# Four units of seven products instead of three in two steps of an FFN, and partial sums added by transfers into DRAM

## The chip, the cores and the metric

The kernel runs on one core of a Trainium2 chip. The core has five engines with queues of their own: TensorE (PE, matrix products), VectorE (DVE), ScalarE (ACT), GpSimd (POOL) and SyncE (SP, which here only issues transfers); transfers are carried by 16 DMA engines. Products are summed in PSUM, everything else lives in SBUF or in DRAM. The metric is the device time of one launch in microseconds (us); less is better.

## What is computed

One layer of an encoder on 256 tokens of width 2048, in fp32: a mixing part (attention heads and a recurrence, behind one input and one output projection), a gated FFN of inner width 5632, and a gated per-layer embedding. The change lies in the FFN:

```
fn = rms_norm(h, g_ffn_pre)
ff = (silu(fn @ w_ffn_gate) * (fn @ w_ffn_up)) @ w_ffn_down
h = h + rms_norm(ff, g_ffn_post)
```

## The kernel before

**Precision.** Every weight product is made of three matmuls on fp32r operands: each operand is split into a high and a low part, and high·high, low·high and high·low are summed. A weight tile (128 x 1024, two blocks of the inner dimension, 512 columns each) is loaded by SP (`wr`, `third`, `lower`, `ple` are its homes, by the ring it comes from), ACT casts its high part (L640, `wh`), DVE takes the low part as the difference (L653, `wl`), and PE uses both (L691 to L693, in this order for each block). The activations hF are split once, at the start of the FFN. High and low parts have rings of four tiles, so DVE can be at most some tiles ahead of PE: how far it is ahead is called its lead in what follows.

**Steps.** The inner width of 5632 is done in 11 steps of 512 columns (f = 0 to 10), in three parts: steps 0 to 3, 4 to 7 and 8 to 10. A step makes two chunks, gate and up, each over eight pairs of blocks k = 0, 2, ..., 14 of fn. ACT then applies silu to the gate (L1725), DVE multiplies by the up product (L1744) and transposes (L340) into a tile `mid`, and 16 small transfers (L350) on POOL, for the last step of a part half of them on SP, arrange it as `mT`. ACT and DVE split it (L312, L314) into `mid0`, `mid1`, `mid2`, one per part. After a part come its down products: four chunks c over the part's inner columns.

**Seven products.** A unit is one pair of k of the gate and the up chunk: eight products of [128 x 128] by [128 x 512], of three matmuls each, 24 matmuls. In steps 2 to 10, for k = 0, 2, 4 (`SEVEN_KS`), the eight are replaced by seven products of sums, in the manner of Strassen and Winograd: 21 matmuls (L702 to L704). They come in three pieces: `four_products` (two tiles of half the usual work, 12 matmuls), begun while the step in front still runs, `two_products` and `one_product`. The sums of weights are DVE's: L588, L592 and L598 in `sum_stream`; the last addend of a block is fetched by an adding transfer on POOL (L609), which waits for the tile's low part. The sums of activations are made once per k (L798, L805 and a split). When the fours of all units of a step are done, `made_of_four` turns the four accumulators into what the rest is added to: a copy on ACT (L750) of one accumulator, then L752, L754, L757 and L759 on DVE.

**Part sums.** The down products of part one are copied to `mid` tiles (ACT, L1832) and stored to a DRAM tensor, part 0. Those of part two are added by DVE (L1825) to what POOL loads back (L1818), and stored to part 1 (L1835). Part three adds its own to `mg`, which SP reloads from part 1 (L1848) near the end of step 10.

**Order.** The program is unrolled. PE's order is written by the groups: the table `FOURS` says at which pair of a step each `four_products` of the next is put, and `TAKEN` when its own twos and ones come. Where the work of the other engines stands in their queues is set by a planner, which keeps a clock for each engine from a table of costs and puts each piece where it expects its inputs; each engine then works through its queue in that order and waits where an input is late.

Of the kernel before, what the change touches and what calls it, by code (L numbers as in the profile page):

```python
# [10 lines left out]
F32 = mybir.dt.float32  # L11
# [5 lines left out]
P = 128  # L17
S = 256
# [22 lines left out]
DOWN_KS = (0, 2, 4, 6)  # L41
OUT = (3, 6, 7, 1)
SEVEN_F = range(2, 11)

SWAPPED = [
    (lambda f: (("w_ffn_gate", f), ("w_ffn_up", f)), SEVEN_F, SEVEN_KS),
    *(
        (
            lambda c: (("w_ffn_down", c), ("w_ffn_down", c + 1)),
# [191 lines left out]
def layer(ctx: ExitStack, tc: tile.TileContext, a: dict, out: bass.AP):  # L241
# [130 lines left out]
    def done(event):  # L372
        event.t = plan.now
# [11 lines left out]
    class Act:  # L385
# [51 lines left out]
    class Group:  # L437
# [76 lines left out]
                fours[self.own[j]] = (*x, self.twos[j])  # L514

    TAKEN = {
        "up3": ("", "01", "2ab"), "down4": ("", "ab0", "12", "3"), "down2": ("", "01", "a"),
    }
    FOURS = {
        ("up0", "up3"): (3, 5, 7), ("up3", "up3"): (2, 3, 4), ("up3", "down4"): (2, 3, 3, 4),  # L520
        ("down4", "down4"): (1, 2, 3, 3), ("down4", "up3"): (1, 2, 3), ("up3", "down2"): (4, 4), ("down2", "down2"): (2, 3),
    }
    fours = {}
# [50 lines left out]
    def sum_stream():  # L574

        for i in sorted(fours):
            for e in fours[i][4].values():
                yield e
            late, last, j, js, _, two = fours[i]
            n, b = first_slot[i], OUT[j]  # L580
            b0 = 2 - 2 * n
            yield ev_load[i]
            yield ev_load[i + 1]
            if n or j == 3:
                yield ev_half_spilled
            Q, R = loaded.pop(i), loaded.pop(i + 1)
            yield dve(N, take=f"T{n}")
            nc.vector.tensor_tensor(  # L588
                out=blocks()[:, b0, :], in0=Q[:, 0, :], in1=Q[:, 1, :], op=ALU.add
            )  # L590
            yield dve(N, take=f"t{j}")
            nc.vector.tensor_tensor(  # L592
                out=blocks()[:, b, :], in0=blocks()[:, b0, :], in1=R[:, 1, :], op=ALU.add
            )
            raws[i] = blocks()[:, b0 : b + 1 : b - b0, :]
            done(ev_raw[i, 2])
            yield dve(N)
            nc.vector.tensor_tensor(out=Q[:, 1, :], in0=Q[:, 1, :], in1=R[:, 1, :], op=ALU.add)  # L598
            raws[i + 1], raws[two] = Q, R
            done(ev_raw[i + 1, 2])  # L600
            done(ev_raw[two, 2])
# [113 lines left out]
    def four_products(group, j, i):  # L715
        (C1, _, _), (C2, _, _) = group.chunks
        kx = group.sevens[j][1]
        ev_s = group.lhs.ev_sums[kx]
        first, last = j == 0, j == len(group.sevens) - 1
        if first:  # L720
            C1.open()
            C2.open()
        plan.main(0, ev_lo[i, 2], group.lhs.ev[kx], ev_s, C1.ready, C2.ready)
        s = group.lhs.sums[kx]
        product(C2.accs[0], s["S1"], i, 0, first, last)
        product(C2.accs[1], s["S2"], i, 1, first, last)
# [58 lines left out]

    def sums_of(lhs, kx, hi, lo):

        lhs.sums[kx] = {
            n: (hi[:, i * P : (i + 1) * P], lo[:, i * P : (i + 1) * P])
            for i, n in enumerate(("S1", "S2", "S7", "S4"))  # L790
        }
        yield lhs.ev[kx]
        yield lhs.ev[kx + 1]
        for j in range(2):
            h, l = lhs.at[kx + j]
            yield dve(S, take=None if j else "T4")
            e, f = (t2["ple"][:, 1, c : c + N] for c in (D // 2, D // 2 + N))
            nc.vector.tensor_tensor(  # L798
                out=e[:, j * S : (j + 1) * S], in0=f32(h), in1=f32(l), op=ALU.add
            )  # L800
        a11, a21, a12, a22 = (e[:, i * P : (i + 1) * P] for i in range(4))
        s1, s2, s7, s4 = (f[:, i * P : (i + 1) * P] for i in range(4))
        for dst, x, y in ((s1, a21, a22), (s2, a11, s1), (s7, a21, a11), (s4, a12, s2)):
            yield dve(P)
            nc.vector.tensor_tensor(out=dst, in0=x, in1=y, op=ALU.subtract)  # L805
        yield from split(hi, lo, f, N, give="T4")
        done(lhs.ev_sums[kx])

    def more_sums():
        for e in hF.ev:  # L810
            yield e
        t2["s"] = t2["pool"].tile([P, 4, N], F32R, tag="mg1", name="s")
        done(ev_unmerged)
        yield from sums_of(hF, 4, t2["s"][:, 0, :], t2["s"][:, 1, :])
        for e in hF.ev_sums.values():
            yield e
        for j in range(4):
            plan.free[f"t{j}"].append(plan.now)
# [183 lines left out]

    HB = 4
    mixT = Act()
    ssr = const.tile([P, S], F32, name="ssr")
    ssa = const.tile([P, S], F32, name="ssa")

    def second_tiles():
        plan.reach(ev_x)
# [145 lines left out]
    def group_rstd(ss, name):  # L1155

        yield pe(0.44, take="sm")
        pb = bank(f"pb_{name}")
        nc.tensor.matmul(pb[:, 0, :], ones, ss, start=True, stop=True)
        rb = const.tile([P, S], F32, name=f"rb_{name}")  # L1160
# [439 lines left out]
    def split_turned(c, mT, hi, lo, nxt, gname):  # L1600
        for b in range(4):
# [10 lines left out]
    parts = [  # L1612
        ctx.enter_context(
            tc.tile_pool(name=f"parts{i}", bufs=1, space=bass.MemoryType.DRAM)
        ).tile([NT, P, D], F32, name=f"part{i}")
        for i in range(2)
    ]
    ev_spilled, ev_all_spilled, ev_back = Event(), Event(), Event()

    def spill_h():  # L1620
# [110 lines left out]
    def mid_tile():  # L1731
        return t2["pool"].tile([P, NT, N], F32, tag="mid", name="mid", bufs=2)
# [79 lines left out]
    def down_post(part, c):  # L1812
        def post(ch):
            sl = slice(c * N, (c + 1) * N)
            if part:
                yield ("pool", COST["move"], None, "mid", None)
                e, here = mid_tile(), Event()
                nc.gpsimd.dma_start(e, parts[0].rearrange("t p d -> p t d")[:, :, sl])  # L1818
                plan.now += COST["landing"]
                done(here)  # L1820
                yield here
            for t in range(NT):
                if part:
                    yield dve(N)
                    nc.vector.tensor_tensor(  # L1825
                        out=e[:, t, :], in0=ch.accs[t], in1=e[:, t, :], op=ALU.add
                    )
                else:
                    yield act(N, take=None if t else "mid")
                    if not t:  # L1830
                        e = mid_tile()
                    nc.scalar.copy(e[:, t, :], ch.accs[t])  # L1832
            ch.release()
            yield ("pool", COST["move"], None, None, None)
            nc.gpsimd.dma_start(parts[part].rearrange("t p d -> p t d")[:, :, sl], e)  # L1835
            plan.now += COST["landing"]
            plan.free["mid"].append(plan.now)
            ev_parts.append((part, c))
        return post
# [35 lines left out]
    for part, (f0, f1) in enumerate(PARTS):  # L1875
        mid = Mid(f"mid{part}")
        last_part = part == len(PARTS) - 1
        for f in range(f0, f1):
            slot = ring()
            g = Chunk(gate_post(f), slot=slot)  # L1880
            u = Chunk(up_post(f, mid, (f - f0) * 4, g, f == f1 - 1), late=(-3 if f == f1 - 1 else -1) * SOON, slot=slot)
            groups.append(Group(
                [(g, "w_ffn_gate", f * N), (u, "w_ffn_up", f * N)], hF, KS,
                SEVEN_KS if f in SEVEN_F else (),
            ))
        ks = [(f0 * 4 + k, k) for k in range(0, (f1 - f0) * 4, 2)]
        for c in range(0, 4, 2):
# [326 lines left out]
```

## Time and profile before

| | |
|---|---|
| median of three runs | 1147.19 us (1147.03 to 1148.57) |
| the profiled execution | 1146.92 us, its span 1145.1 us |
| FFN gate and up, down, in the trace | about 360 to 1036 us |
| matmul records | 5193, of which 15 fp32 matmuls are recorded twice |
| TensorE clock granted | 0.998 |
| memory traffic | 249.65 MB read, 9.44 MB written |

A row of the profile names line, engine, operation, output and inputs, shape and count; times are us from the start of the span, and in a timeline the start, then the duration. Idle time before an instruction stands in brackets with what ended it. Matmuls overlap, so their price is the distance of starts and not the duration of a row.

### The profile page before, as it was taken

To read this page: it belongs to the slowest core of one execution; us is meant where nothing else is said; L and a number is where in the kernel's file an instruction comes from. 1 tells how busy PE (TensorE), PEld (TensorE's weight loads), DVE (VectorE), ACT (ScalarE), POOL (GpSimd) and SP (SyncE) were. 2 spreads that over 40 slices of the span, in tenths; PEclk is the share of its full clock that TensorE was granted. 3 is DMA by queue.
4 is the path that set the end of the run, shared out by engine and by line. 5 is a ranking of instruction groups with operands and counts; after the bars stand their busy time and mean duration, and the time that the engine had idled before them with its cause. 6 is when DMAs were issued, how large, how long until landed. Compare 5 with 4: busy or idle time off the path is not lost.

```text
span 1145.1 us, 15184 instructions
## 1 busy us (share of the span) xinstructions
PE 1136.3 (99%) x5193; PEld 944.7 (82%) x5193; DVE 932.7 (81%) x1174; ACT 727.2 (63%) x959; POOL 147.7 (13%) x234
## 2 busy tenths in 40 slices
PE   9999999999999999999999999999999999999997
PEld 8888888888888888888888888888888888788886
DVE  6678697888468779898987898999988888888574
ACT  6877877875447645665666566556555565577564
POOL 0000000000000032132010133222111303100200
PEclk9999999999999999999999999999999999999999
DMA  9867566546685996887977777897797777977861
GB/s 317 295 191 217 182 193 200 175 150 203 220 300 175 314 295 207 228 243 214 292 259 220 257 225 214 249 274 240 257 317 246 216 249 240 278 237 257 240 218 74
DMA packets 110558, 268.49 MB, mean 234 GB/s; under 512 B 36304, under 2 KB 43216, under 8 KB 109072
## 3 DMA queue, kind: packets, MB, share of 16 engines
q1 hardware_dynamic: 96304, 243.17, 63.3%
q0 software_dynamic: 13744, 24.00, 10.9%
q8 instruction: 40, 0.66, 0.2%
q10 hardware_dynamic: 432, 0.35, 0.1%
q14 instruction: 38, 0.31, 0.1%
HBM read 249.65 MB, written 9.44 MB: 226 GB/s over the span
## 4 chain that ended last, share of the span: by engine, by line
PE 93%; DVE 3%; DMA 2%; ACT 2%; issue 1%; SPq 0%; POOL 0%; ACTq 0%; DVEq 0%; POOLq 0%
PE acc L693 23%; PE acc L692 23%; PE acc L691 23%; PE acc L704 6%; PE acc L703 6%; PE acc L702 6%; DVE wl L653 1%; PE tr L331 1%; DMA mg<-part 1%; ACT wh L640 1%; DMA sq<-ev 0%; PE warm L2123 0%; PE pg L362 0%; PE pg L363 0%; PE pg L361 0%
## 5 line engine op out<-in xcount | busy, mean ns | idle before, releaser
L653 DVE TENSOR_TENSOR wl<-wr,wh 128x1024 fp32r<-128x1024 f32 (+1 forms) x300 | 358.6, 1209 | 100.7 <-ACT wh L640 98.9
L640 ACT CAST wh<-wr 128x1024 fp32r<-128x1024 f32 (+1 forms) x300 | 310.8, 1043 | 171.8 <-PE acc L692 114.2
L350 POOL DMA_DIRECT2D mT<-mid x164 | 96.3, 597 | 607.7 <-DMA lower<-in_w_ffn_up 400.7
L692 PE MATMUL acc<-wh,hT_mix_lo 128*128 128x512 f32 x420 | 163.6, 390 | 0.3 <-DVE hT_mix_lo L320 0.3
L691 PE MATMUL acc<-wh,hT_mix_hi 128*128 128x512 f32 x420 | 163.7, 390 | 0.0
L693 PE MATMUL acc<-wl,hT_mix_hi 128*128 128x512 f32 x420 | 163.4, 389 | 0.0
L693 PE MATMUL acc<-wl,hT_hi 128*128 128x512 f32 x320 | 124.6, 390 | 0.0
L691 PE MATMUL acc<-wh,hT_hi 128*128 128x512 f32 x316 | 124.4, 394 | 0.0
L692 PE MATMUL acc<-wh,hT_lo 128*128 128x512 f32 x316 | 123.1, 390 | 0.0
L640 ACT CAST wh<-ple 128x1024 fp32r<-128x1024 f32 (+1 forms) x68 | 68.2, 1008 | 77.2 <-DVE ple L592 47.3
L692 PEld LDWEIGHTS acc<-wh,hT_mix_lo 128*128 128x128 f32 x420 | 78.9, 188 | 17.2 <-DVE hT_mix_lo L320 1.0
L691 PEld LDWEIGHTS acc<-wh,hT_mix_hi 128*128 128x128 f32 x420 | 78.9, 188 | 16.3
L693 PEld LDWEIGHTS acc<-wl,hT_mix_hi 128*128 128x128 f32 x420 | 78.8, 188 | 16.3
L653 DVE TENSOR_TENSOR wl<-ple,wh 128x1024 fp32r<-128x1024 f32 (+1 forms) x68 | 79.2, 1164 | 10.1 <-ACT wh L640 9.7
L693 PEld LDWEIGHTS acc<-wl,hT_hi 128*128 128x128 f32 x320 | 60.1, 188 | 13.0 <-DVE wl L653 0.3
L692 PEld LDWEIGHTS acc<-wh,hT_lo 128*128 128x128 f32 x316 | 59.4, 188 | 11.6
L691 PEld LDWEIGHTS acc<-wh,hT_hi 128*128 128x128 f32 x316 | 59.4, 188 | 11.5
L609 POOL DMA_DIRECT2D ple<-in_w_ffn_up x27 | 24.0, 890 | 164.6 <-DVE wl L653 123.2
L640 ACT CAST wh<-third 128x1024 fp32r<-128x1024 f32 x32 | 33.6, 1051 | 13.4 <-PE acc L692 7.9
L691 PE MATMUL acc<-wh,hT_ffn_hi 128*128 128x512 f32 x104 | 40.9, 393 | 0.0
L692 PE MATMUL acc<-wh,hT_ffn_lo 128*128 128x512 f32 x104 | 40.6, 390 | 0.1
L693 PE MATMUL acc<-wl,hT_ffn_hi 128*128 128x512 f32 x104 | 40.5, 390 | 0.0
(439 smaller groups left out, 2455.6 us busy)
## 6 DMA issues: line engine op xcount, KB each, us to landing
wr<-in_w_in SPq DMA_DIRECT2D x77, 512.0 KB, 4.5
wr<-in_w_ffn_gate SPq DMA_DIRECT2D x73, 512.0 KB, 5.3
wr<-in_w_ffn_down SPq DMA_DIRECT2D x55, 512.0 KB, 6.0
wr<-in_w_ffn_up SPq DMA_DIRECT2D x51, 512.0 KB, 4.8
wr<-in_w_out SPq DMA_DIRECT2D x32, 512.0 KB, 4.3
wr<-in_w_ple_gate SPq DMA_DIRECT2D x32, 512.0 KB, 4.6
lower<-in_w_ffn_up SPq DMA_DIRECT2D x21, 512.0 KB, 6.1
lower<-in_w_ffn_down SPq DMA_DIRECT2D x17, 512.0 KB, 5.5
```

What stands on the lines that cost most here:

```text
L331: nc.tensor.transpose(tr[:, b, t * P : (t + 1) * P], e[:, t, sl], ident)
L350: (nc.gpsimd if i in pool else nc.sync).dma_start(dst[32 * j : 32 * j + 32, :, :, i, :], src[32 * i : 32 * i + 32, :, :, j, :],)
L609: nc.gpsimd.dma_start(dst, src, accum_op=ALU.add)
L640: nc.scalar.copy(his[i][:, 0 : src.shape[1], :] if n == 2 else his[i][:, j, :], src)
L653: nc.vector.tensor_tensor(out=los[i][:, m, :], in0=src, in1=f32(his[i][:, m, :]), op=ALU.subtract)
L691: nc.tensor.matmul(accs[t], hi[:, sl], his[i][:, j, :], start=st, stop=False, **group)
L692: nc.tensor.matmul(accs[t], lo[:, sl], his[i][:, j, :], start=False, stop=False, **group)
L693: nc.tensor.matmul(accs[t], hi[:, sl], los[i][:, j, :], start=False, stop=sp, **group)
L702: nc.tensor.matmul(dst, x[0], wh, start=start, stop=False, skip_group_check=seeded)
L703: nc.tensor.matmul(dst, x[1], wh, start=False, stop=False, skip_group_check=seeded)
L704: nc.tensor.matmul(dst, x[0], wl, start=False, stop=stop, skip_group_check=seeded)
```

## The change

The units of k = 6 of steps 5 and 9 are made of seven products too. The sums of hF for k = 6 get a tile `more`, which takes a place where small statistics of the mixing part lay before (`ssr`, `ssa`, `rb_*`, now together in `quad`). A step with four units takes its fours at pairs 2, 2, 3, 3 of the step in front instead of 2, 3, 4, and begins those of the next step at pairs 1, 2, 3 instead of 2, 3, 4. For the fourth unit the block sums take another slot, so the order of blocks within a tile is turned there (`turn`).

The four down products of part two are no longer added by DVE: ACT copies them to `mid`, as in part one, and POOL's transfer adds them in DRAM to what part one has stored. One DRAM tensor `parted` takes the place of the two.

```diff
+FOUR_F = (5, 9)
 SWAPPED = [
     (lambda f: (("w_ffn_gate", f), ("w_ffn_up", f)), SEVEN_F, SEVEN_KS),
+    (lambda f: (("w_ffn_gate", f), ("w_ffn_up", f)), FOUR_F, (6,)),
...
     TAKEN = {
-        "up3": ("", "01", "2ab"), "down4": ("", "ab0", "12", "3"), "down2": ("", "01", "a"),
+        "up3": ("", "01", "2ab"), "up4": ("", "ab0", "12", "3"), "down4": ("", "ab0", "12", "3"), "down2": ("", "01", "a"),
     }
     FOURS = {
         ("up0", "up3"): (3, 5, 7), ("up3", "up3"): (2, 3, 4), ("up3", "down4"): (2, 3, 3, 4),
+        ("up3", "up4"): (2, 2, 3, 3), ("up4", "up3"): (1, 2, 3), ("up4", "down4"): (1, 2, 3, 3),
+        ("up4", "up4"): (1, 2, 3, 3), ("down4", "up4"): (1, 2, 3, 3), ("up4", "down2"): (2, 3),
...
-            raws[i] = blocks()[:, b0 : b + 1 : b - b0, :]
+            raws[i] = blocks()[:, min(b, b0) : max(b, b0) + 1 : abs(b - b0), :]
...
-        product(C2.accs[0], s["S1"], i, 0, first, last)
-        product(C2.accs[1], s["S2"], i, 1, first, last)
+        turn = int(OUT[j] < 2 - 2 * first_slot[i])
+        product(C2.accs[0], s["S1"], i, turn, first, last)
+        product(C2.accs[1], s["S2"], i, 1 - turn, first, last)
...
+        more = const.tile([P, 4, S], F32R, tag="quad", name="more")
+        yield from sums_of(hF, 6, *(more[:, :, b : b + P] for b in (0, P)))
...
-    ssr = const.tile([P, S], F32, name="ssr")
-    ssa = const.tile([P, S], F32, name="ssa")
+    quad = const.tile([P, 4, S], F32, tag="quad", name="quad")
+    ssr, ssa = quad[:, 0, :], quad[:, 1, :]
...
-            if part:
-                yield ("pool", COST["move"], None, "mid", None)
-                e, here = mid_tile(), Event()
-                nc.gpsimd.dma_start(e, parts[0].rearrange("t p d -> p t d")[:, :, sl])
-                plan.now += COST["landing"]
-                done(here)
-                yield here
             for t in range(NT):
-                if part:
-                    yield dve(N)
-                    nc.vector.tensor_tensor(
-                        out=e[:, t, :], in0=ch.accs[t], in1=e[:, t, :], op=ALU.add
-                    )
-                else:
-                    yield act(N, take=None if t else "mid")
-                    if not t:
-                        e = mid_tile()
-                    nc.scalar.copy(e[:, t, :], ch.accs[t])
+                yield act(N, take=None if t else "mid")
+                if not t:
+                    e = mid_tile()
+                nc.scalar.copy(e[:, t, :], ch.accs[t])
             ch.release()
             yield ("pool", COST["move"], None, None, None)
-            nc.gpsimd.dma_start(parts[part].rearrange("t p d -> p t d")[:, :, sl], e)
-            plan.now += COST["landing"]
+            to = parted.rearrange("t p d -> p t d")[:, :, sl]
+            if part:
+                nc.gpsimd.dma_start(to, e, accum_op=ALU.add)
+                plan.now += ADDED
+            else:
+                nc.gpsimd.dma_start(to, e)
+                plan.now += COST["landing"]
...
-        nc.sync.dma_start(back[n, t], (spill if n == "h" else parts[1])[t])
+        nc.sync.dma_start(back[n, t], (spill if n == "h" else parted)[t])
...
-                SEVEN_KS if f in SEVEN_F else (),
+                SEVEN_KS + (6,) if f in FOUR_F else SEVEN_KS if f in SEVEN_F else (),
```

The planner's clocks run differently with this, so other work changes its place as well, from step 4 on; the program has 6 matmuls fewer. Three places follow.

DVE in step 10, around the sums that follow the fours of the down products of part three (L752 to L759, after the change L757 to L764), the low parts (L653, then L657) of the last tiles of step 10 beside them, and the up product's post (L1744 and L340, then L1747 and L342). Before:

```order
L314 TENSOR_TENSOR mid2l_7832<-mT,mid2h_7831 128x512 x2
L653 TENSOR_TENSOR wl<-third,wh 128x1024
L653 TENSOR_TENSOR wl<-wr,wh 128x1024 x2
L752 TENSOR_TENSOR u<-u,acc_8286 128x512
L754 TENSOR_TENSOR u<-u,acc_8284 128x512
L757 TENSOR_TENSOR acc_8286<-acc_8285,u 128x512
L759 TENSOR_TENSOR acc_8285<-acc_8285,u 128x512
L653 TENSOR_TENSOR wl<-wr,wh 128x1024 x2
L1744 SCALAR_TENSOR_TENSOR mid<-acc_7866,rstd_f,mid 128x512
L1744 SCALAR_TENSOR_TENSOR mid<-acc_7867,rstd_f,mid 128x512
L340 STREAM_TRANSPOSE mid<-mid 128x1024
```

After the change:

```order
L316 TENSOR_TENSOR mid2l_7869<-mT,mid2h_7868 128x512 x2
L657 TENSOR_TENSOR wl<-wr,wh 128x1024
L757 TENSOR_TENSOR u<-u,acc_8290 128x512
L759 TENSOR_TENSOR u<-u,acc_8288 128x512
L762 TENSOR_TENSOR acc_8290<-acc_8289,u 128x512
L764 TENSOR_TENSOR acc_8289<-acc_8289,u 128x512
L657 TENSOR_TENSOR wl<-third,wh 128x1024
L657 TENSOR_TENSOR wl<-wr,wh 128x1024 x2
L657 TENSOR_TENSOR wl<-lower_3672,wh 128x1024
L1747 SCALAR_TENSOR_TENSOR mid<-acc_7833,rstd_f,mid 128x512
L1747 SCALAR_TENSOR_TENSOR mid<-acc_7834,rstd_f,mid 128x512
L342 STREAM_TRANSPOSE mid<-mid 128x1024
```

The sums stand one low part earlier: the first one behind them (from `third`) is now that of the last up tile of step 10, which stood ahead of them before. The post has four low parts between itself and the sums, where it had two.

POOL from the down products of part two to the moves of step 8: loads and stores of the part sums, late weight additions for steps 8, 9 and 10 (into `ple`), moves of mT. Before:

```order
L1818 DMA mid<-part_98 128x2x512 x2
L1835 DMA part_101<-mid 128x2x512
L609 DMA ple<-in_w_ffn_up 128x512
L1835 DMA part_101<-mid 128x2x512
L609 DMA ple<-in_w_ffn_up 128x512 x2
L1818 DMA mid<-part_98 128x2x512 x2
L1835 DMA part_101<-mid 128x2x512 x2
L609 DMA ple<-in_w_ffn_up 128x512 x3
L350 DMA mT<-mid 32x8x32 x16
```

After the change:

```order
L1827 DMA parted<-mid 128x2x512 x2
L613 DMA ple<-in_w_ffn_up 128x512 x3
L1827 DMA parted<-mid 128x2x512 x2
L613 DMA ple<-in_w_ffn_up 128x512 x4
L352 DMA mT<-mid 32x8x32 x9
L613 DMA ple<-in_w_ffn_up 128x512
L352 DMA mT<-mid 32x8x32 x7
```

The loads are gone, the stores of a pair of chunks stand together, a fourth late addition follows them, and one for the step after stands between the ninth and the tenth move of mT.

PE in step 4, from the second tile of the third unit of fours of step 5 (on `s`, the sums of hF for k = 4; L702 to L704 are the seven products, L691 to L693 the plain ones, after the change L706 to L708 and L695 to L697). Before:

```order
L702 MATMUL acc_5524<-wh,hT_mix_hi 128x512
L703 MATMUL acc_5524<-wh,hT_mix_lo 128x512
L704 MATMUL acc_5524<-wl,hT_mix_hi 128x512
L702 MATMUL acc_5525<-wh,s 128x512
L703 MATMUL acc_5525<-wh,s 128x512
L704 MATMUL acc_5525<-wl,s 128x512
L691 MATMUL acc_5173<-wh,hT_mix_hi 128x512
L692 MATMUL acc_5173<-wh,hT_mix_lo 128x512
L693 MATMUL acc_5173<-wl,hT_mix_hi 128x512
```

After the change:

```order
L706 MATMUL acc_5527<-wh,hT_mix_hi 128x512
L707 MATMUL acc_5527<-wh,hT_mix_lo 128x512
L708 MATMUL acc_5527<-wl,hT_mix_hi 128x512
L706 MATMUL acc_5528<-wh,s 128x512
L707 MATMUL acc_5528<-wh,s 128x512
L708 MATMUL acc_5528<-wl,s 128x512
L706 MATMUL acc_5529<-w,more 128x512
L707 MATMUL acc_5529<-w,more 128x512
L708 MATMUL acc_5529<-w,more 128x512
L706 MATMUL acc_5530<-w,more 128x512
```

The fourth unit (on `more`) follows the third at once, and the second follows the first in the same way: four weight tiles of six matmuls stand back to back, where each unit of fours had tiles of twelve matmuls behind it.

More of the change, by code (lines that the diff above doesn't have):

```diff
@@ L786, in sums_of @@
     def sums_of(lhs, kx, hi, lo):
[L788 to L791, printed above, removed]
+        if len(hi.shape) == 2:
+            hi, lo = (x.rearrange("p (b q) -> p b q", q=P) for x in (hi, lo))
+        lhs.sums[kx] = {n: (hi[:, i, :], lo[:, i, :]) for i, n in enumerate(("S1", "S2", "S7", "S4"))}
         yield lhs.ev[kx]
@@ L805, in sums_of @@
             nc.vector.tensor_tensor(out=dst, in0=x, in1=y, op=ALU.subtract)
-        yield from split(hi, lo, f, N, give="T4")
+        yield from split(hi, lo, f.rearrange("p (b q) -> p b q", q=P), N, give="T4")
         done(lhs.ev_sums[kx])
@@ L1159, in group_rstd @@
         nc.tensor.matmul(pb[:, 0, :], ones, ss, start=True, stop=True)
-        rb = const.tile([P, S], F32, name=f"rb_{name}")
+        rb = quad[:, 2 if name == "rec" else 3, :]
         yield act(S, SQRT, give="sm")
@@ L1611, in layer @@
     ).tile([NT, P, D], F32, name="h_spill")
[L1612 to L1617, printed above, removed]
+    parted = ctx.enter_context(
+        tc.tile_pool(name="parted", bufs=1, space=bass.MemoryType.DRAM)
+    ).tile([NT, P, D], F32, name="parted")
     ev_spilled, ev_all_spilled, ev_back = Event(), Event(), Event()
```

## Prediction

> **What bounds the kernel now.** I read the page first: busy time by engine, and the chain of waits.
>
> ```profile
> span 1145.1 us, 15184 instructions
> ...
> PE 1136.3 (99%) x5193; PEld 944.7 (82%) x5193; DVE 932.7 (81%) x1174; ACT 727.2 (63%) x959; POOL 147.7 (13%) x234
> ...
> PE 93%; DVE 3%; DMA 2%; ACT 2%; issue 1%; SPq 0%; POOL 0%; ACTq 0%; DVEq 0%; POOLq 0%
> ```
>
> TensorE sets the time: 99% busy, 93% of the chain. So the time changes by two things alone: the number of matmuls, and the holes in PE's stream that other engines make. The price of a matmul comes from the timeline of PE in step 10:
>
> ```profile
> 975.61 0.39 PE L704 MATMUL acc<-wl,sums 128*128 128x512 f32 x1
> 975.84 0.39 PE L691 MATMUL acc<-wh,hT_mix_hi 128*128 128x512 f32 x1
> ...
> 978.56 0.39 PE L691 MATMUL acc<-wh,hT_mix_hi 128*128 128x512 f32 x1
> ...
> 979.01 0.39 PE L693 MATMUL acc<-wl,hT_mix_hi 128*128 128x512 f32 x1
> ```
>
> From 975.84 to 978.56 PE starts the 12 matmuls of one weight tile: 2.72 us, 0.2267 us each, whatever the 0.39 of a single row says. Holes: from step 0 to the end of the FFN I find one of note, in the down products of part three.
>
> ```profile
> 996.47 0.39 PE L703 MATMUL acc<-wh,sums 128*128 128x512 f32 x1
> 997.03 0.50 PE L704 MATMUL acc<-wl,sums 128*128 128x512 f32 x1 [0.18 <-DVE wl L653]
> 997.37 0.40 PE L702 MATMUL acc<-wh,sums 128*128 128x512 f32 x1
> ...
> 998.32 0.39 PE L703 MATMUL acc<-wh,mid2l 128*128 128x512 f32 x1
> 998.77 0.50 PE L704 MATMUL acc<-wl,mid2h 128*128 128x512 f32 x1
> 999.10 0.40 PE L702 MATMUL acc<-wh,sums 128*128 128x512 f32 x1
> ...
> 994.79 0.69 DVE L314 TENSOR_TENSOR mid2l<-mT,mid2h 128x512 fp32r<-128x512 f32 x1 [3.10 <-ACT mid2h L312]
> ...
> 981.48 9.73 DMA mg<-part
> ...
> 991.23 2.81 DMA mT<-mid
> ```
>
> Starts 0.56 (996.47 to 997.03), 0.34, 0.45 (998.32 to 998.77) and 0.33 apart instead of 0.2267: 1.68 - 4 x 0.2267 = 0.77 us, and some 0.85 with the 0.24 steps beside them. The chain names its origin: the reload of `mg` takes from 981.48 to 991.23, the last transfer that turns the activations of step 10 (mT) goes behind it, and DVE stands 3.10 us for it.
>
> So DVE is the engine to watch. What matters is not its share but its lead: by how much the low part of a weight tile (L653) is done before PE starts on the tile.
>
> ```profile
> 653.00:695.00 42.00, 42.00 (x188) 34.76 (x186) 37.80 (x44) 25.61 (x29) 12.00 (x19) 1.00 0.73 223
> 902.00:944.00 42.00, 42.00 (x187) 34.80 (x186) 36.42 (x41) 24.41 (x28) 12.06 (x19) 1.00 0.73 223
> ...
> 646.46 1.22 DVE L653 TENSOR_TENSOR wl<-wr,wh 128x1024 fp32r<-128x1024 f32 x1 [1.49 <-ACT wh L640]
> ...
> 653.52 0.39 PE L691 MATMUL acc<-wh,hT_mix_hi 128*128 128x512 f32 x1
> ...
> 713.55 1.22 DVE L653 TENSOR_TENSOR wl<-third,wh 128x1024 fp32r<-128x1024 f32 x1
> ...
> 714.72 0.39 PE L691 MATMUL acc<-wh,hT_mix_hi 128*128 128x512 f32 x1
> ```
>
> The first two rows are windows of 42 us over steps 5 and 9 (columns: sum, PE, PEld, DVE, ACT, POOL, clock, DMA share, GB/s): DVE works 37.8 and 36.4 us of each. The tile that PE starts at 653.52 was ready at 646.46 + 1.22 = 647.68, 5.8 us ahead; the ring of four tile buffers allows no more. The one started at 714.72, in step 6, was ready at 714.77: no lead at all, and no hole only because `wl` is read by the third matmul of the tile.
>
> **The change, part by part.** *Matmuls.* Steps 5 and 9 each turn one unit of eight products (24 matmuls) into seven (21): 2 x 3 = 6 matmuls fewer, 6 x 0.2267 = **-1.36 us**. Nothing excludes it, since PE streams without holes there. The Trainium skill, "TensorE: Matmul & The Clock Gate", section "Back-to-back issue gap", puts a sustained matmul of 512 columns at about 131 ns; by it the six would be worth 0.79 us, estimated. The trace disagrees (226.7 ns), and the trace decides.
>
> *DVE's new work.*
>
> ```profile
> L592 DVE TENSOR_TENSOR ple<-ple,lower 128x512 f32<-128x512 f32 x38 | 26.2, 690 | 1.2 <-DMA lower<-in_w_ffn_up 0.3
> L588 DVE TENSOR_TENSOR ple<-wr 128x512 f32<-128x512 f32 x37 | 25.1, 678 | 0.0
> L598 DVE TENSOR_TENSOR wr<-wr,lower 128x512 f32<-128x512 f32 x31 | 21.2, 685 | 0.0
> ...
> L1825 DVE TENSOR_TENSOR mid<-acc,mid 128x512 f32<-128x512 f32 x8 | 5.2, 683 | 0.0
> ...
> L805 DVE TENSOR_TENSOR ple<-ple 128x128 f32<-128x128 f32 x12 | 2.9, 286 | 0.1
> L798 DVE TENSOR_TENSOR ple<-hT_mix_hi,hT_mix_lo 128x256 f32<-128x256 f32 x6 | 2.4, 415 | 0.0
> ```
>
> A unit of seven adds, over the pair it replaces, three sums (0.68 + 0.69 + 0.69 = 2.05), one more full low part (1.22, as at 646.46) and half a one (0.54 over the half tile): 3.8 us, while PE needs 0.68 less. Step 5's window becomes 37.8 + 3.8 = 41.6 of 41.3 us. That is more than full, but part of it is done in step 4, whose tiles lead by nearly the whole 5.8, and steps 6 and 10 begin their own fours one pair earlier. Going through the new order tile by tile with these durations, I find the lead never under 0.8 us in steps 4 to 6 and 8 to 9: at the four tiles done back to back (1.8), after the sums of the four (0.8 to 1.4, where the tile's first two matmuls give 0.45 more), and at the up product's end. I take 0; bounds 0 and, if the lead is gone in both places, the 5.2 of the first slow rival. The sums of activations for k = 6 (two of L798, four of L805, one split of 0.68: 2.7 us) fall before step 2, with the ring's lead to cover them: 0.
>
> *Step 10, up product.* Here the order puts the sums that follow the fours (L752 to L759) one tile earlier.
>
> ```profile
> 974.45 1.06 ACT L640 CAST wh<-wr 128x1024 fp32r<-128x1024 f32 x1 [0.30 <-PE acc L703]
> 975.41 0.57 ACT L750 COPY u<-acc 128x512 f32<-128x512 f32 x1
> ...
> 972.86 2.54 DVE L653 TENSOR_TENSOR wl<-wr,wh 128x1024 fp32r<-128x1024 f32 x2
> 976.02 0.69 DVE L752 TENSOR_TENSOR u<-u,acc 128x512 f32<-128x512 f32 x1 [0.61 <-ACT u L750]
> ...
> 978.14 0.69 DVE L759 TENSOR_TENSOR acc<-acc,u 128x512 f32<-128x512 f32 x1
> 978.74 2.35 DVE L653 TENSOR_TENSOR wl<-wr,wh 128x1024 fp32r<-128x1024 f32 x2
> 981.00 1.41 DVE L1744 SCALAR_TENSOR_TENSOR mid<-acc,rstd_f,mid 128x512 f32<-128x512 f32 x2
> ```
>
> The sums cannot begin before PE ends the fours (975.61) and ACT copies (to 975.98), so they fill DVE until 978.74 in either order. Before, the tile that PE starts at 978.56 was done by 975.40, ahead of them. Now its low part comes behind them: 978.74 + 1.22 = 979.96, while PE wants it at 979.01. Cost **+0.95 us**; behind it wait DVE's next low parts, of which each needs 1.13 (half of the 2.35 less overlap) against PE's 1.36 to 2.72, so the delay is paid once. Bounds: 0, if the copy and the sums run early, and 1.5, if the copy comes one cast (0.57 or more) later.
>
> *What comes late next.* The up product's post (L1744, then the transpose) stands behind four low parts instead of two: 978.74 + 4 x 1.13 = 983.3 instead of 981.0, and the transfers of mT go with it. Before, they waited for the reload of mg anyway, until 991.23; that reload is issued by SP behind a weight load which waits for a low part one place later, about +1.1. So mT lands 1.1 later, of which 0.95 is already in PE's own delay, and one low part more stands ahead of the waiting sums. The hole of 0.85 at 997 may close (-0.85) or grow by the whole 1.1 to 1.3; I take **+0.2**.
>
> *Part two's down products.*
>
> ```profile
> 811.68 1.80 POOL L1818 DMA_DIRECT2D mid<-part  x2
> 825.82 0.73 POOL L1835 DMA_DIRECT2D part<-mid  x1 [12.34 <-DVE mid L1825]
> ...
> DMA to landing us min/median/max: 3.2/6.1/7.1
> ...
> DMA to landing us min/median/max: 4.0/5.0/8.7
> ...
> L1832 ACT COPY mid<-acc x8: 589/589/590, 570.8 to 612.2; 128x512 f32<-128x512 f32 x8
> ```
>
> Away go four loads of the partial sum and eight additions on DVE (8 x 0.683 = 5.5 us); in come eight copies on ACT (8 x 0.589 = 4.7 us, and ACT is busy 24 to 26 us in the windows of 42) and four stores that add in DRAM. DVE's gain is no gain in time, as PE has no hole there. No row shows an adding store into DRAM. Below, it is the plain store of the same 512 KB (first landing row: 3.2 to 7.1); above, two of the adding loads of 256 KB (second row, 8.7 each): 17 us. Nearest is the plain store plus a read, so some 9. The buffer is wanted again by the gate of the step after next, over 30 us later, and the sum by the reload of mg 100 us later: 0 either way. The Trainium skill, "DMA: Bandwidth & Descriptors", section "Anatomy of one DMA — SWDGE (gpsimd) path", gives about 2 us and bytes at 436 GB/s, so an estimated 3.2 for a plain 512 KB; the plain stores' median of 6.1 says more, and by either nothing waits.
>
> *Sum:* -1.36 + 0.95 + 0.2 = **-0.2 us** on the profiled execution of 1146.92 (span 1145.1 and 1.8 around it), which lies 0.27 under the median of 1147.19. On that median: **1147.0**.
>
> **Rivals.** *Both waits stay away* (faster): the copy runs early, the hole at 997 closes. -1.36 - 0.85 = -2.2: 1145.0 by the median. For it speaks that DVE gets relief in part two; against it, that the sums hang on PE's own fours. Even so it is at the edge of 0.2% (2.3 us), which is about what a measurement of this kernel can tell from no change.
>
> *DVE becomes the bound in steps 5 and 6, 9 and 10* (slower): the extra 3.8 per step is not taken up by the lead. Of the 4.2 us that DVE was free in the window of step 5, some 0.6 were waits for the copy L750 and, as at 712 in step 6, 1.7 for mT; such waits stay. Then 3.8 + 0.7 (PE's shorter time) meets 1.9 of real room: 2.6 us a step, 5.2 in all, less 1.36: about 1151. It decides once the lead at the entry to step 6 is under 2.6. For it: the place at 714.72 without lead. Against it: steps 4 and 8 enter full, and that place's wait for mid1 now stands behind three more low parts.
>
> *The adding stores are slow* (slower): two adding transfers at a time, holding the 16 engines so that weight tiles come late. It takes a landing beyond 30 us or so, and would cost perhaps one tile's arrival, 5 us: 1151. Against it: the DMA share of 0.73 in both windows shown, and weight tiles that are fetched several tiles ahead.
>
> *mT waits behind POOL* (slower): in steps 5 and 9 one late weight addition now stands between the moves of mT, seven of them behind it. If POOL stands there half as long as it stood for DVE before 825.82 (12.34), the split of the activations on ACT and DVE comes 6 us late, less a lead of 2 to 4: +2 to 4, so 1149 to 1150. Against it: by the new order the low part it waits for is done when the ninth move is.
>
> *The change doesn't do what it says* is excluded for the matmuls, by their count.
>
> **Numbers.** Forecast, no change: 0.62, its own range 1145.5 to 1148.9 (1147.19 - 1.36 with no wait, 1147.19 - 1.36 + 1.5 + 1.3 with both at their upper bound, and 0.3 for the spread of runs). Faster rival 0.08; DVE bound 0.18; adding stores 0.05; mT 0.07. So faster by over 0.2% 0.08, within 0.62, slower 0.30. The range reaches to the faster rival and over half of the slow ones: 1144.7 to 1150.9.
>
> **What would show it.** PE's rows: 6 fewer matmuls, 0.2267 apart. In step 10, a hole of about 1 us at the third matmul of the last up tile, put down to DVE's low part, and the mid2 wait about 1 us later. No hole in 395 to 420, none in 625 to 735 and 870 to 960: holes there, ended by L653, make the DVE rival right and me wrong; holes ended by the cast L640 behind a DMA mean late weights; a DVE wait for mid1h of more than 3 us means the moves of mT. The adding stores' landing row should read 6 to 17.

## The result, and the profile after

The changed kernel takes 1161.33 us (median of 4 runs, 1160.92 to 1161.62) against 1147.11 for the one before: a ratio of 1.0118, 95% interval 1.0103 to 1.0133. The two medians lie 14.2 us apart; by the ratio, which is formed from the runs and not from the medians, the loss is 13.5 us. Both are well outside the range. The profiled execution has a span of 1159.4 us, 14.3 more than before. Its page:

```profile
span 1159.4 us, 15192 instructions
...
PE 1139.0 (98%) x5187; PEld 944.2 (81%) x5187; DVE 936.5 (81%) x1181; ACT 734.0 (63%) x970; POOL 148.3 (13%) x232
...
PE 91%; DMA 3%; DVE 2%; ACT 2%; issue 1%; POOL 0%; SPq 0%; ACTq 0%; DVEq 0%
```

The six matmuls are gone (5187 for 5193), DVE has only 3.8 us more to do in all, and in the chain transfers went from 2% to 3%. So I look for holes and add up, for PE's starts more than 0.3 us apart in the FFN, what exceeds 0.2267:

| place (us, after) | before | after |
|---|---|---|
| 681 and 689, steps 5 and 6 | 0 | 0.86 |
| 930, step 9 | 0 | 1.61 |
| 982, step 10's last up tile | 0 | 1.10 |
| 997 to 1014, first down products of part three | 0.79 | 11.62 |

That is 15.2 against 0.8; less 1.36 for the matmuls it gives +13.0. The rest of the 14.3 lies ahead of step 4, where the order is the same (0.7 before the FFN), and in steps of under 0.3. One place holds most of it. PE's timeline there:

```profile
992.73 0.39 PE L695 MATMUL acc<-wh,mid2h 128*128 128x512 f32 x1
992.95 0.39 PE L696 MATMUL acc<-wh,mid2l 128*128 128x512 f32 x1
1000.33 0.80 PE L697 MATMUL acc<-wl,mid2h 128*128 128x512 f32 x1 [6.99 <-DVE wl L657]
1000.93 0.63 PE L695 MATMUL acc<-wh,mid2h 128*128 128x512 f32 x1
1001.35 0.63 PE L696 MATMUL acc<-wh,mid2l 128*128 128x512 f32 x1
```

PE stands 7.4 us (992.95 to 1000.33) for a low part, and then starts a matmul only every 0.43 us. Who is late? The timelines of DVE, ACT and SP, and SP's waits from 970 to 995 (us in all, times, longest):

```profile
988.04 1.18 DVE L657 TENSOR_TENSOR wl<-lower,wh 128x1024 fp32r<-128x1024 f32 x1
998.45 0.69 DVE L592 TENSOR_TENSOR ple<-third 128x512 f32<-128x512 f32 x1 [9.23 <-DMA third<-in_w_ffn_down]
...
996.40 1.04 ACT L644 CAST wh<-wr 128x1024 fp32r<-128x1024 f32 x1 [8.05 <-DMA wr<-in_w_ffn_down]
...
964.49 10.75 SPq L552 DMA_DIRECT2D wr<-in_w_ffn_down  x3
989.25 0.33 SPq L1843 DMA_DIRECT2D mg<-parted  x1
989.62 0.42 SPq L552 DMA_DIRECT2D wr<-in_w_ffn_down  x1
990.10 0.43 SPq L552 DMA_DIRECT2D third<-in_w_ffn_down  x1
990.57 0.76 SPq L552 DMA_DIRECT2D lower<-in_w_ffn_down  x1
991.37 1.08 SPq L552 DMA_DIRECT2D wr<-in_w_ffn_down  x2
992.50 0.50 SPq L1843 DMA_DIRECT2D mg<-parted  x1
993.33 13.46 SPq L352 DMA_DIRECT2D mT<-mid  x8
...
SPq L1843 <- DVE wl L657: 13.8, 1, 13.8
```

DVE and ACT stand 8 to 9 us for weights. The weights were asked for only at 989.62 and after, because SP stood 13.8 us at the instruction ahead of them: the first reload of `mg`, issued at 989.25. It waits for a low part, and the one that ends then is the row above: 988.04 + 1.18 = 989.22, `wl<-lower`. Before the change the same reload went out 21 us earlier, right behind the loads ahead of it:

```profile
968.16 0.33 SPq L1848 DMA_DIRECT2D mg<-part  x1
```

Why should a reload of `mg` wait for a weight tile? The code tells. `lower_tile` (L277) takes homes 3 and 4 of its ring of five from a tile with the tag `mg0`, the memory of the first half of `mg`. The ring is dealt out in order (L2077 after, `(3, 4, 0, 1, 2)[n % RING]`; the last two tiles are fixed). Each additional unit uses one home more: 49 in all instead of 47. So the phase moves by two:

```
before: step 10: 3 4 0   down products of part three: 1 2 | 0 1
after:  step 10: 0 1 2   down products of part three: 3 4 | 0 1
```

Before, homes 3 and 4 were last read for step 10; now they hold weights of part three's own down products, read at 988. The reload's place in SP's queue stayed ahead of the five weight loads, so these came late, and so did the moves of `mT` behind them. The chain of waits shows the latter:

```profile
992.50 13.69 DMA mg<-parted
...
1006.21 1.94 DMA mT<-mid
```

With seven transfers asked for within 4 us, this reload takes 13.69 us (9.73 before), and the last move of `mT` goes behind it. SP's waits (from 940 to 1010; us in all, times, longest) say how: SP asks for that move only when the reload has landed.

```profile
SPq L352 <- DMA mg<-parted: 3.0, 2, 2.7
```

It stood 2.1 us for it before the change. The two transfers write different tiles (tags `mg1` and `mt`); why the one waits for the other, no run shows. DVE's split of `mT` follows at 1008.9, and PE stops again at 1010.8 (2.38 in all).

The half speed after the hole is read from the windows (sum, PE, PEld, DVE, ACT, POOL, clock, DMA share, GB/s):

```profile
993.00:1000.30 7.30, 0.34 (x2) 0.00 (x0) 1.85 (x3) 1.99 (x2) 0.44 (x1) 0.82 1.02 350
1000.30:1004.80 4.50, 4.47 (x11) 3.56 (x12) 3.54 (x4) 1.04 (x1) 0.00 (x0) 0.53 1.07 378
1004.80:1010.00 5.20, 4.60 (x21) 3.45 (x19) 1.10 (x2) 1.75 (x3) 0.00 (x0) 1.00 0.86 132
```

The granted clock is 0.53 for 4.5 us, which costs another 2.1 us; the holes of under 2 us at 930 and 982 were followed by no such stretch. The Trainium skill, "TensorE: Matmul & The Clock Gate", section "What's actually happening", states that the clock falls to half after an idle window of about 3.4 us and returns after about as long a busy one. This trace agrees: 7.4 idle, then 4.5 slow. The figure of 3.4 as the least idle time is not borne out by the runs below: in e6 a hole of 2.4 us is followed by 3.2 us at a granted clock of 0.50, while in e12 one of 2.3 us is followed by no slow stretch.

The theory from here on, **A**: the memory shared by `mg` and homes 3 and 4. Its rivals: **B**, the adding stores; **C**, and for the lesser holes **D**, DVE with too much to do.

### The profile page after: what moved, and what is told of

It is laid out like the page before. It is cut to its first block, busy times and chain, and to the rows that moved or that the text cites. A ratio compares the mean times of both kernels' runs of the same rounds, so it can differ in the third digit from the quotient of the medians.

```text
span 1159.4 us, 15192 instructions
## 1 busy us (share of the span) xinstructions
PE 1139.0 (98%) x5187; PEld 944.2 (81%) x5187; DVE 936.5 (81%) x1181; ACT 734.0 (63%) x970; POOL 148.3 (13%) x232
## 4 chain that ended last, share of the span: by engine, by line
PE 91%; DMA 3%; DVE 2%; ACT 2%; issue 1%; POOL 0%; SPq 0%; ACTq 0%; DVEq 0%
PE acc L697 23%; PE acc L696 23%; PE acc L695 23%; PE acc L706 6%; PE acc L708 6%; PE acc L707 6%; DMA mT<-mid 1%; DMA mg<-parted 1%; DVE wl L657 1%; PE tr L333 1%; ACT wh L644 1%; POOL mT L352 0%; DMA av<-in_w_rg_i 0%; PE pg L364 0%; PE pg L365 0%
## 5 line engine op out<-in xcount | busy, mean ns | idle before, releaser
L657 DVE TENSOR_TENSOR wl<-wr,wh 128x1024 fp32r<-128x1024 f32 (+1 forms) x300 | 358.7, 1209 | 91.5 <-ACT wh L644 90.4
L697 PE MATMUL acc<-wl,hT_mix_hi 128*128 128x512 f32 x408 | 159.1, 390 | 2.3 <-DVE wl L657 2.2
L696 PE MATMUL acc<-wh,hT_mix_lo 128*128 128x512 f32 x408 | 159.0, 390 | 0.3 <-DVE hT_mix_lo L322 0.3
L695 PE MATMUL acc<-wh,hT_mix_hi 128*128 128x512 f32 x408 | 159.0, 390 | 0.0
L644 ACT CAST wh<-ple 128x1024 fp32r<-128x1024 f32 (+1 forms) x71 | 72.8, 1029 | 84.2 <-DVE ple L596 57.1
L697 PE MATMUL acc<-wl,hT_hi 128*128 128x512 f32 x320 | 124.6, 390 | 0.0
L695 PE MATMUL acc<-wh,hT_hi 128*128 128x512 f32 x316 | 124.4, 394 | 0.0
L697 PEld LDWEIGHTS acc<-wl,hT_mix_hi 128*128 128x128 f32 x408 | 76.6, 188 | 19.4 <-DVE wl L657 3.6
L657 DVE TENSOR_TENSOR wl<-ple,wh 128x1024 fp32r<-128x1024 f32 (+1 forms) x71 | 84.2, 1189 | 8.9 <-ACT wh L644 8.5
L695 PEld LDWEIGHTS acc<-wh,hT_mix_hi 128*128 128x128 f32 x408 | 76.6, 188 | 15.6
L697 PEld LDWEIGHTS acc<-wl,hT_hi 128*128 128x128 f32 x320 | 60.1, 188 | 13.3 <-DVE wl L657 0.5
L695 PEld LDWEIGHTS acc<-wh,hT_hi 128*128 128x128 f32 x316 | 59.4, 188 | 11.4
L695 PE MATMUL acc<-wh,hT_ffn_hi 128*128 128x512 f32 x104 | 40.9, 393 | 0.1
L697 PE MATMUL acc<-wl,hT_ffn_hi 128*128 128x512 f32 x104 | 40.5, 390 | 0.0
```

Source lines behind the costliest of these rows:

```text
L644: nc.scalar.copy(his[i][:, 0 : src.shape[1], :] if n == 2 else his[i][:, j, :], src)
L657: nc.vector.tensor_tensor(out=los[i][:, m, :], in0=src, in1=f32(his[i][:, m, :]), op=ALU.subtract)
L695: nc.tensor.matmul(accs[t], hi[:, sl], his[i][:, j, :], start=st, stop=False, **group)
L696: nc.tensor.matmul(accs[t], lo[:, sl], his[i][:, j, :], start=False, stop=False, **group)
L697: nc.tensor.matmul(accs[t], hi[:, sl], los[i][:, j, :], start=False, stop=sp, **group)
```

## The experiments

Times are medians, and ratios are to the kernel before on the same chip, with 95% intervals. Holes are read from the one profiled execution of each run. In e1, e5, e6 and e8 it took 1150.84, 1148.36, 1151.08 and 1155.21 us, 1.6 to 3.2 above the median, so the holes given for these four need not be those of a middling execution.

**e1, the adding stores alone.** Edit, on the changed kernel (and no sums for k = 6):

```diff
-FOUR_F = (5, 9)
+FOUR_F = ()
```

> Only part two's adding stores are kept; steps 5 and 9 have three units of seven, as before, and there is no sum for k = 6. Theory A (the memory of mg: two more weight homes are used in all, so the ring of five homes ends in another phase, the two homes that share memory with mg's first half are the ones still read by the down products at 988 us, and SP's queue stands 13.8 us behind mg's reload): the number of homes is that of before, the reload does not wait, so within 1.5 us of before, 1145.7 to 1148.7. Theory B (the adding stores are slow, or the reload waits for them): the loss is here, +8 us or more. Theory C (DVE has too much to do with the additional units): no loss, at most a gain of 1 us.

1149.22 us, 1.0012 (1.0002 to 1.0021). The large loss is not here, so B falls, but the time is half a us above A's bound. The profile has one new hole, 4.57 us at 998; its chain of waits says why:

```profile
981.05 12.01 DMA mg<-parted
993.08 2.83 DMA mT<-mid
```

The planner had put both reloads close together (977.57 and 981.05); the second took 12.0 us instead of 9.7, and a move of `mT` goes behind it. e10 tests this.

**e2, the fourth units alone.** Part two's `down_post` and its tensors as before the change.

> Only the fourth units are kept; part two's sums are added by DVE as before and stored to a tensor of their own. Theory A: the wait of mg's reload is there, so nearly the whole loss, 1157 to 1163. Theory B: no loss, 1145 to 1148. Theory C: the whole loss or more, since DVE has its eight additions back: 1161 to 1167.

1161.65 us, 1.0118 (1.0103 to 1.0133): the whole loss, with the same wait of 13.8 us of SP at the reload. The time lies in A's range and in C's alike. What tells them apart is this wait, and that the time is the changed kernel's (1161.33) though DVE has its eight additions back: no sign of C.

**e3, the ring in another phase.** One edit on the changed kernel:

```diff
-        lower[i] = (3, 4, 0, 1, 2)[n % RING] if ...
+        lower[i] = (3, 4, 0, 1, 2)[(n + 3) % RING] if ...
```

> The changed kernel, with the ring of five weight homes begun three places on, so that the last four are those of before and the two homes in mg's memory are free by step 10. Nothing else is edited. Theory A: mg's first reload goes out without waiting (near 970 instead of 989), the hole of 7.4 us at 1000 and the half-speed matmuls behind it go, and what stays are the holes at 681 and 690 (0.9), 930 (1.6) and 982 (1.1): 1148 to 1152. Theories B and C: 1159 to 1163, since neither the stores nor DVE's work is touched.

1150.98 us, 1.0029 (1.0018 to 1.0040): by the ratios, 10.2 of the 13.5 us come back from a number in a subscript. Units, sums and stores are unchanged, and from 360 to 1000 us the source lines follow one another on DVE, ACT, POOL and SP as in the changed kernel. SP's timeline:

```profile
964.03 10.75 SPq L552 DMA_DIRECT2D wr<-in_w_ffn_down  x3
974.96 0.33 SPq L1843 DMA_DIRECT2D mg<-parted  x1
977.08 0.33 SPq L552 DMA_DIRECT2D wr<-in_w_ffn_down  x1
981.72 0.33 SPq L552 DMA_DIRECT2D third<-in_w_ffn_down  x1
```

The reload goes out right behind the loads ahead of it, and the weight loads behind it 8 to 13 us earlier than in the changed kernel (the first, into `wr`, at 977.08 for 989.62, the one into `lower` at 982.10 for 990.57). The holes left are 681 and 689 (0.84), 930 (1.45), 982 (1.10) and 1.89 at 1000.

**e4, the reloads later in the queue.** The same wait, but with the weight loads ahead of it:

```diff
-            plan.add(reload("mg", 0), plan.clk["pe"] + 15.0)
-            plan.add(reload("mg", 1), plan.clk["pe"] + 23.0)
+            plan.add(reload("mg", 0), plan.clk["pe"] + 30.0)
+            plan.add(reload("mg", 1), plan.clk["pe"] + 32.0)
```

> The changed kernel, with both reloads of mg put later in SP's queue, behind the moves of mT for step 10; homes, units and stores as in the change. Theory A: the five weight loads and mT no longer stand behind the reload, so the hole at 1000 goes as in the run with the other ring phase, 1147 to 1152, unless the reload is then late for the first down chunk's end (a hole of up to 3 us near 1020). Theory B: if the reload is slow in itself, the hole moves to 1020 and stays at 7 us or more. Theory C: 1159 to 1163.

1150.14 us, 1.0022 (1.0013 to 1.0032). The hole at 1000 is gone; 0.93 turned up at 1023, as A allowed. Two unlike cures, one of the wait and one of what stands behind it, give the same.

**e9, the fourth unit in step 5 alone** (`FOUR_F = (5,)`).

> The changed kernel with the fourth unit in step 5 alone; step 9 has three, as before. One home more than before is used in all, so the ring ends one place off: the last unit but two of the down products reads home 3, in mg's memory, again. Theory A: the first reload of mg waits until 985 or later though nothing in steps 8 to 10 has more work than before, and most of the loss is there, 1155 to 1161. Rival D (the additional work of the steps): half of the loss or less, since half the units are gone, 1146 to 1154.

1154.88 us, 1.0061 (1.0048 to 1.0075): just under A's range and just above D's, so the time alone does not separate them; the place of the loss does. The ring is one place off, and SP waits 7.7 us at the reload, until 987.29. Four of the five weight loads stand ahead of it here, but the second reload (988.14, 9.43 us) and the last move of `mT` behind it do not, and PE's hole is 7.61 at 1002. Nothing in steps 8 to 10 has more work than before, so a unit in step 5 shows in the down products, some 310 us later. How much of the 7.61 is the unit's this run does not tell: e1, without any unit, has 4.57 in the same place, by the same second reload.

**e7, the kernel before with its second reload later.** On the kernel before, only `23.0` to `30.0` for the second reload.

> The kernel before, with its second reload of mg put behind the moves of mT for step 10, and nothing else. If the hole of 0.79 at 997 of before comes from the reload that a transfer of mT stands behind, it goes: 0.9993 of before. If mT is late by itself, nothing changes.

1146.21 us, 0.9987 (0.9978 to 0.9996). No hole is left in the FFN at all, and SP no longer stands for the reload at a move of `mT`. So the 0.79 that I had called "may close" hung on that reload.

**e10, the adding stores and the second reload later.** e1 with the edit of e7.

> Only part two's adding stores (as in e1), with the second reload of mg behind the moves of mT (as in e7). The hole of 4.6 us at 998 of e1 is the last move of mT waiting for a reload that takes 12.0 us beside the other one; with this reload later it goes, and what stays is the price of the adding stores by themselves. Theory A: that price is nothing, so the time of e7, 0.998 to 0.9995 of before. Theory B: above 1.001.

1146.70 us, 0.9991 (0.9982 to 1.0000); the hole at 998 shrank from 4.57 to 0.65. The adding stores by themselves cost nothing that these runs can tell. They land in 7.4 to 9.0 us in the changed kernel:

```profile
L1827 POOL DMA_DIRECT2D parted<-mid x4: 1205/1216/1223, 820.9 to 861.7; - x4
...
DMA to landing us min/median/max: 7.4/7.6/9.0
```

**e5, ring, second reload and the split of mT.** For the lesser holes. ACT's cast of `mT` in step 9 waited for step 8's moves, here in the changed kernel (ACT, DVE, then PE):

```profile
926.12 0.62 ACT L314 CAST mid2h<-mT 128x512 fp32r<-128x512 f32 x1 [4.60 <-DMA mT<-mid]
...
926.78 0.69 DVE L316 TENSOR_TENSOR mid2l<-mT,mid2h 128x512 fp32r<-128x512 f32 x1 [3.81 <-ACT mid2h L314]
...
929.99 0.50 PE L697 MATMUL acc<-wl,hT_mix_hi 128*128 128x512 f32 x1 [1.34 <-DVE wl L657]
```

The edit, with e3's phase and `30.0` for the second reload alone:

```diff
-            {0: 12.0, 9: 6.0}.get(f, 3.0)
+            {0: 12.0, 4: 8.0, 8: 8.0, 9: 6.0}.get(f, 3.0)
```

> The changed kernel with three edits: the other ring phase of e3; only the second reload of mg put later (behind the moves of mT); and the split of mT of steps 4 and 8 planned 8 us after its transfers instead of 3. By the order the sums of the down fours in step 10 then stand behind the low part of the last up tile again. Theory A with its two lesser places (ACT waits 4.6 us for step 8's mT, which is why PE stops at 930; the sums stand one low part too early, which is why it stops at 982): no hole over 0.3 us between 360 and 1040, so -1.36 for the matmuls and -0.79 for before's own hole: 0.9981 of before, 1145 to 1146.5. Rival D (DVE is full in steps 5, 6, 9 and 10 and the holes at 681, 690 and 930 are its doing): these holes stay, 1147.5 to 1149.

1146.49 us, 0.9996 (0.9987 to 1.0004): level with before, where A had 0.9981 and no hole. The holes at 681, 689 and 930 are gone, but others came: 740 and 757 (0.88), 983 (1.05, now behind step 9's cast, which waits 1.95 for its own `mT`), 999 (0.90). The one at 689 (0.34 to 0.45) is in all seven profiles that have the unit in step 5 and the split of step 4 as it was, and in none of the three with that split later (e5, e6, e8). The one at 681 is less firm: it is also missing in e12, which leaves that split alone.

**e6, both reloads and the split later**, the ring as in the change.

> The changed kernel with the reloads of mg both later (as in e4) and the split of mT of steps 4 and 8 later, ring phase as in the change. Theory A: the holes at 681, 690, 930 and 982 go, that of 0.9 at 1023 (reloads late for the first down chunks' end) stays: 1145.5 to 1147.5. Rival D: 1148.5 to 1150.5.

1149.49 us, 1.0017 (1.0008 to 1.0026), a miss: the holes at 681, 930 and 982 went, but one of 3.8 us came at 1016, where the chain shows a weight load of 10.6 us beside the two reloads of 1 MB issued at 994; lesser ones came at 740 (0.4) and 997 (0.9). The time lies in D's range, but the holes that D named are gone.

**e8, the split of step 9 later as well.** e5 with `4: 6.0, 8: 6.0, 9: 12.0`.

> The three edits of e5 (ring phase, second reload of mg behind mT, split of mT later), with the split of steps 4 and 8 at 6 us instead of 8 and that of step 9 at 12 instead of 6, so that ACT's copy for the down fours of step 10 no longer stands behind a cast that waits for mT (1.95 us at 978 in e5). Theory A: the hole of 1.05 at 983 goes, those at 740 and 757 (0.9) go or stay: 0.998 to 0.999 of before, 1145.2 to 1146.4. Rival D: as e5, 1146.5 or more.

1152.06 us, 1.0032 (1.0023 to 1.0041), a clear miss. ACT's copy no longer stands behind a cast that waits for `mT`, but from 983 on PE loses 6.3 us. PE's stop of 3.3 us there, until 986.56, is ended by DVE's split of `mT`. ACT's cast for it was done at 983.2, but in DVE's queue the split now stands behind the up product's post and a sum of weights:

```profile
982.62 1.43 DVE L1747 SCALAR_TENSOR_TENSOR mid<-acc,rstd_f,mid 128x512 f32<-128x512 f32 x2 [0.26 <-PE acc L697]
984.09 1.25 DVE L342 STREAM_TRANSPOSE mid<-mid 128x1024 f32<-128x1024 f32 x1
985.26 0.65 DVE L592 TENSOR_TENSOR ple<-third 128x512 f32<-128x512 f32 x1
985.83 0.68 DVE L316 TENSOR_TENSOR mid2l<-mT,mid2h 128x512 fp32r<-128x512 f32 x1
```

The rest is a stretch of matmuls 0.43 us apart behind that hole. The edit puts this split later, and its place in DVE's queue fits the loss; no run isolates it.

**e11 and e12, the first reload earlier.** Both have e3's phase, the first reload at `0.0` and the second at `30.0`; e12 has `8: 8.0` for the split of step 8 besides.

> The changed kernel with the ring phase of e3, the first reload of mg put 15 us earlier in SP's queue (the other phase allows it) and the second behind the moves of mT; the split of mT as in the change. Theory A: the holes at 681, 689 (0.85), 930 (1.5) and 982 (1.1) stay, none over 0.3 at 985 to 1040: 3.45 - 0.79 - 1.36 = +1.3 us, 1.0005 to 1.002 of before.

> As e11, and the split of mT of step 8 planned 8 us after its transfers instead of 3; nothing else. Theory A (ACT's wait for mT of step 8, and through the order the place of the sums in step 10): the holes at 930 and at 982 go, 2.6 us less than e11, 0.998 to 0.9995 of before. Rival D (DVE is full in steps 9 and 10): as e11, or the holes turn up elsewhere between 900 and 985.

1150.26 us, 1.0024 (1.0015 to 1.0033), and 1149.56 us, 1.0018 (1.0009 to 1.0027). Both are above what A had for them, and the two intervals overlap, so the times do not separate the pair; the profiles do, at one place. The edits differ by one number. In e11 ACT waits at 926.42, in e12 it does not:

```profile
926.42 0.62 ACT L314 CAST mid2h<-mT 128x512 fp32r<-128x512 f32 x1 [5.03 <-DMA ple<-in_w_ffn_up]
```

```profile
926.82 0.61 ACT L314 CAST mid2h<-mT 128x512 fp32r<-128x512 f32 x1
```

The first fence is e11's, the second e12's. (Of the several waits of the cast, e11's row names a late addition, which goes out between the moves of `mT`; in the changed kernel the row above named a move.) The hole at 928 (2.04 us) goes with it, so that hole is this wait's and not DVE's load. But at 983 there are 2.17 us for e11's 2.03: in e12 PE waits for a split of `mT` behind the sums of the fours, and these stand behind a weight that came late (ACT waited 1.42 us for its load at 977). Of the 2.6 us expected, the medians show 0.7. By the words of its expectation, with a hole left between 900 and 985, D is not excluded by this run.

## Why the prediction was wrong

**The step that failed** is the one on what comes late next in step 10: "that reload is issued by SP behind a weight load which waits for a low part one place later, about +1.1", with +0.2 taken. I had followed the second reload alone, as the chain of before names it. The first, which waits for nothing there, I took as it stood: its wait is at nothing in the sum and in no rival, since I never asked whose memory it writes. The change lengthens a list, the list sets a ring's phase, and the phase decides which weights lie in that memory. What the runs showed in its place: SP stands 13.8 us at the first reload, five weight loads are asked for 8 to 13 us later than in e3 and `mT` after them, and the place costs 10.8 us more than before, where the term was +0.2. e3 and e4 show it from two sides. The order alone could not tell it, since the reload stands in much the same place of SP's queue; what it waits for, and whose memory that is, would have.

**Right in mechanism, off in size:**
- The sums of the fours one low part earlier: +0.95 foreseen, at the third matmul of the last up tile. Measured 1.10:

```profile
982.16 0.50 PE L697 MATMUL acc<-wl,hT_mix_hi 128*128 128x512 f32 x1 [0.83 <-DVE wl L657]
...
980.29 0.69 DVE L764 TENSOR_TENSOR acc<-acc,u 128x512 f32<-128x512 f32 x1
980.89 1.22 DVE L657 TENSOR_TENSOR wl<-third,wh 128x1024 fp32r<-128x1024 f32 x1
```

- The moves of `mT` on POOL, given 0.07 as a rival: it did occur, at 681 (0.41) and 930 (1.61). The price of "+2 to 4" was about right for the two together (with the sum's -0.2 it makes 1149.0 to 1151.0, not the 1149 to 1150 written there), but the late addition between the moves was the lesser part of it. It held the queue for 0.6 us (913.39 to 913.99); the up product's post ended 3.8 us later than before (transposes done at 907.2 for 903.4) and the last move was asked for 3.8 us later, while ACT reached its cast only 2.2 us later (921.5 for 919.3). Of the moves' landing of 5.8 and 7.1 us in the chain, I have not separated the cause.

**Right:**
- The matmuls: six fewer, and the rate between holes unchanged. What the six are worth by themselves no run isolates. The account of holes does not speak against the -1.36: e5 has 2.8 us of them and e10 0.65, which less 1.36 makes 0.8 us or 0.0007, and their ratios are 0.9996 and 0.9991. But each ratio is known to 0.0009 only, and the two profiled executions lie 1.4 us apart, of which holes of over 0.3 us explain this 0.8.
- Part two's sums: adding stores landed inside the bounds of 6 to 17, nothing waited for them, and DVE's relief gave no time (e2).
- DVE is not the bound, though the prediction's own sign for it came: holes at 681, 689 and 930, ended by the low part (L657). The sign did not tell a full DVE from one that stands for `mT`, which it did for 2.6 us in step 5 and 3.8 in step 9. The holes went in e5, where the split of `mT` came later and DVE's work was no less. So 41.6 of 41.3 us looked full, but the lead could carry it. That rival held the largest chance of the slow ones.

**What stays open.** A version that keeps the fourth units and beats e7. Moving a reload or a split closed some holes and opened others further on (e5, e6, e8); I put this down to the planner, whose clocks shift the work behind it, but no run isolates it. The fastest kernel by its ratio is e7 (0.9987), without the change; its interval overlaps those of e10 and e5.

## What to carry to other kernels

Before a change adds an entry to any list, find what is dealt out by position in it: buffers, rings, lanes. A shifted phase moves a wait to code that the diff never touches. A queue that issues in order makes one such wait everybody's: for each transfer on a shared queue, ask who last read the memory that it writes, and put transfers with slack (here the second reload, which before the change goes out at 981 and is read no earlier than 1012) behind those without.

## What had not been expected of the hardware

A reload of 1 MB took 9.7 us before the change, 12.0 beside a second one (e1) and 13.7 beside five weight loads; in the changed kernel the first, asked for ahead of them, took 5.0. A move of `mT`, 32 KB, was asked for only when the reload in front of it had landed: SP stood 2.1 us for it before the change, 2.7 after it and 4.2 in e1. And an idle stretch of 7.4 us on TensorE is paid for once more, with 2.1 us at a granted clock of 0.53.
